# Gate and convolution tiles of a state-space group in turns, a planner that keeps TensorE to one kind of pass, and attention's output gates through DRAM between heads

## The chip, the cores and the metric

The kernel runs on one NeuronCore of a Trainium2 chip. The metric is device time in microseconds (us), from the start to the end of one execution. Engines are named as in the profile: PE is TensorE, DVE is VectorE, ACT is ScalarE, POOL is GpSimd, SP is SyncE, which issues most DMAs.

## The reference, cut to what matters

One layer of a hybrid encoder: 16 learned rows are put ahead of 512 tokens, and an attention branch and a bidirectional state-space (SSD) branch run on the same normalized rows. Every input-side column comes from one projection with `w_in`.

```python
u = rmsnorm(h, norm_w)                                   # 528 x 1024
q_lat, kv_lat, k_rope, g_attn, z, xbc, dt_raw, merge = split(u @ w_in)
y_a = mla_branch(q_lat, kv_lat, k_rope, ...)             # 16 heads, softmax over 528 keys
y_a = (y_a * silu(g_attn)) @ w_attn_proj
xbc = silu(conv5(xbc) + conv_b)                          # x, B, C of 4 groups of 8 heads
y = ssd_fwd(x, dt, B, C) + ssd_bwd(x, dt, B, C) + d_skip * x
y = rmsnorm(y * silu(z))                                 # by group
y_s = y @ w_ssd_proj
gates = sigmoid(merge)                                   # 2 x 1024 columns
h = h + (gates[0] * y_a + gates[1] * y_s) @ w_out
out = rmsnorm(h, final_norm_w)[16:]
```

## The kernel before, in words

Everything is float32. A projection is split in three: weights and inputs are cut into a high and a low part of type `fp32r`, and hi*hi, hi*lo and lo*hi are added up in PSUM (`proj`). Such a matmul goes through PE in one pass. A few matmuls of the SSD part (`cb`, `st`, `yo`, `yd`, `ssq`) are plain float32; each shows up in the trace as two MATMUL records. Transposes are a third kind (`tr`, `pt`, `yt`, `rb`).

The work is written as generators, "units". A projection unit loads 512 KB of weights (`wr`), lets ACT cast the high part (`wh`) and DVE form the low part (`wl`), then runs 24 matmuls of 512 columns into one PSUM bank, or 48 of 270 for a convolution tile. The units that matter here:

- `silu_tile` makes a gate tile `z` (SSD groups: `z_units`; attention: `g_fill`).
- `conv_tile` makes B, C or one of four x tiles of a group (`in_units`): a projection into a two-bank PSUM tile of tag `d`, of which there are two, then five DVE operations over 528 columns.
- `proj_unit` multiplies a finished group by `w_ssd_proj` into `ysacc`.
- `merge_s` makes the SSD branch's output gate (`ms`), `merge_a` attention's (`ma`); each is a projection unit with a tanh behind it.
- `mix_unit` multiplies attention's output by `w_attn_proj`, applies the two gates and splits the sum for `out_unit`, the last projection.

The SSD groups run as main work: `ssd_tok`, `ssd_cb`, `ssd_state`, `ssd_cross`, `ssd_y`, `ssd_weight` and the epilogue `group_epi` (gating, norm, split of the group). Attention runs head by head: `score_gen` does four score tiles (`sc`, 24 matmuls), the row maximum on DVE, the exponential on ACT and the scaling on DVE; `value_gen` transposes the probabilities (`pt`, 20), splits them (`pT`, ACT then DVE) and multiplies them by the values (`o`, 9).

What fills PE around the main work stands in `queue`; `drive` opens up to four units of it at a time, in the queue's order as far as their conditions allow. This recording is then put in order by `_Recorder.order` (L164), a list scheduler with modelled durations: of all operations that can go it takes the one with the earliest modelled start, and among equals the one recorded first (`rank`). It charges 95 ns (`SWITCH`) whenever PE changes between a plain float32 matmul (`four`) and anything else. The instructions are emitted in that order, each engine runs its own in order, and all carry the line of `rec.emit` (L261).

The lines that the change touches: L210 to 212, the choice of the next operation; L1507 to 1512, which queue for each group first all z units, then all `proj_unit`s of the group before, then all convolution tiles of the next group; L1283 to 1292, `merge_a`, which leaves each gate in an SBUF slot; L1536, which queues the eight `merge_a` units for when head 13 (`GATES`) is done.

Of the kernel before, what the change touches and what calls it, by code (L numbers as in the profile page):

```python
# [9 lines left out]
F32 = mybir.dt.float32  # L10
# [6 lines left out]
P = 128  # L17
D = 1024
NM = 16
NX = 512  # L20
# [23 lines left out]
LAG = 1250.0  # L44
MAHEAD, TOKC, CBC = 2, 2, 1
MAINS, OPEN, LOOK = 24, 4, 20
QLATE, GATES, SPLIT = 1, 13, 99


WPOOL, WPOOLB = 2, 4  # L50
# [41 lines left out]
class _Recorder:  # L92
# [15 lines left out]
    @classmethod  # L108
    def region(cls, ap):
        step = ap.ap[0][0]  # L110
        if ap.name == "cum_rows":
            return 0, 1, [(0, 1)]
        p0, f0 = divmod(ap.offset, step) if step else (0, ap.offset)
        dims = [(st, n) for st, n in ap.ap[1:] if st and n > 1]
        if "PSUM" in str(getattr(ap, "space", "")):
            end = f0 + sum(st * (n - 1) for st, n in dims)
            return 0, P, [(f0 // cls.BANK * cls.BANK, (end // cls.BANK + 1) * cls.BANK)]
        dims.sort(reverse=True)
        spans = [(f0, f0 + 1)]
        for k, (st, n) in enumerate(dims):  # L120
            rest = sum(a * (b - 1) for a, b in dims[k:]) + 1
            inner = sum(a * (b - 1) for a, b in dims[k + 1:]) + 1
            if inner >= st or n * len(spans) > 32:
                return p0, p0 + ap.shape[0], [(a, a + rest) for a, _ in spans]
            spans = [(a + st * m, a + st * m + 1) for a, _ in spans for m in range(n)]
        return p0, p0 + ap.shape[0], spans
# [31 lines left out]
        o.tiles = sorted({n for n, _ in rs + ws if n in self.tags})  # L158
        self.ops.append(o)

    AHEAD, SPARE = 4, 2
    TO_PE, TO_REST, SWITCH = 155.0, 35.0, 95.0

    def order(self):  # L164


        ops = self.ops
        left, ready = [0] * len(ops), [0.0] * len(ops)
        for o in ops:
            o.succs = []  # L170
        for o in ops:
            for k in o.preds:
                ops[k].succs.append(o)
            left[o.i] = len(o.preds)
        count, last, held, place, turn, passed = {}, {}, set(), {}, {}, {}
        for o in ops:
            for n in o.tiles:
                if n not in count:
                    tag = self.tags[n]
                    place[n] = turn.get(tag, 0)  # L180
                    turn[tag] = place[n] + 1
                count[n] = count.get(n, 0) + 1
        turn = {t: 0 for t in turn}
        passed = {t: set() for t in turn}
        free = {t: [0.0] * self.cap[t] for t in turn}
        clk = {e: 0.0 for e in ("PE", "DVE", "ACT", "POOL", "SP")}
        cand = {e: [] for e in clk}
        port = lock = wire = 0.0
        four = False
        for o in ops:  # L190
            if not left[o.i]:
                cand[o.eng].append(o)

        def when(o):
            t = max(clk[o.eng], ready[o.i], lock if o.eng == "POOL" else port if o.both else 0.0)
            for n in o.tiles:
                if n not in held:
                    tag = self.tags[n]
                    f, ahead = free[tag], place[n] - turn[tag]
                    if not f or ahead > self.AHEAD or (ahead > 0 and len(f) <= self.SPARE):  # L200
                        return None
                    t = max(t, f[0])
            return t

        out = []
        while len(out) < len(ops):
            best = None
            for q in cand.values():
                for o in q:
                    t = when(o)  # L210
                    if t is not None and (best is None or (t, o.rank) < best[:2]):
                        best = (t, o.rank, o)
            if best is None:
                raise RuntimeError(("no operation can go", len(out)))
            t, _, o = best
            cand[o.eng].remove(o)
            o.start = t
            for n in o.tiles:
                if n not in held:
                    held.add(n)  # L220
                    tag = self.tags[n]
                    free[tag].pop(0)
                    passed[tag].add(place[n])
                    while turn[tag] in passed[tag]:
                        turn[tag] += 1
            more = 0.0
            if o.eng == "PE" and o.four != four:
                four, more = o.four, self.SWITCH
            elif o.both:
                lock = t + o.occ  # L230
            elif o.eng == "POOL":
                port = t + o.occ + 60.0
            if o.eng == "SP":
                clk["SP"] = t + 420.0
                wire = max(wire, t + 1600.0) + o.dur
                end = wire + o.extra
            else:
                clk[o.eng] = t + o.occ + more
                end = t + o.dur + more
            for n in o.tiles:  # L240
                last[n] = max(last.get(n, 0.0), end + 40.0)
                count[n] -= 1
                if not count[n]:
                    f = free[self.tags[n]]
                    f.append(last[n])
                    f.sort()
            for s in o.succs:
                to = end + (self.TO_PE if s.eng == "PE" else self.TO_REST) if s.preds[o.i] else t + o.occ
                ready[s.i] = max(ready[s.i], to)
                left[s.i] -= 1  # L250
                if not left[s.i]:
                    cand[s.eng].append(s)
            out.append(o)
        self.span = max(o.start + o.dur for o in out)
        return sorted(out, key=lambda o: (o.start, o.i))
# [98 lines left out]
def hybrid_block_kernel(ctx, tc, a, out):  # L354
    nc = tc.nc
    scr = nc.dram_tensor("cum_rows", (2, NC, 32, P), F32, kind="Internal").ap()

    cp = ctx.enter_context(tc.tile_pool(name="cp", bufs=1))
    rp = ctx.enter_context(tc.tile_pool(name="rp", bufs=WRAW))
# [438 lines left out]
    def has(*keys):  # L798
        return lambda: all(k in done for k in keys)
# [478 lines left out]
        done.add(("ms", m))  # L1278

    w_ap = a["w_attn_proj"][0].rearrange("(k p) m -> p k m", p=P)  # L1280
    mx_, gates, ysp = {}, {}, {}

    def merge_a(m):  # L1283
        w = yield from w_cols(O_MA + m * P)
        ps = yield from proj(w, u_src, QRY)
        wdone()
        yield
        z = slot([P, NX], name="ma")
        A.activation(z, ps, AF.Tanh, scale=0.5)
        drop("m")  # L1290
        gates[m] = z
        done.add(("ga", m))

    def split_y(p):
# [7 lines left out]

    def mix_unit(m):
        w = yield from weights(lambda raw: [(raw, w_ap[:, :, m * P:(m + 1) * P])], KD, P)
        ps = yield from proj(w, [ysp[p] for p in range(KD)], slice(0, NX))
        wdone()
        yield has(("ga", m), ("ms", m))
        z = gates.pop(m)
        V.scalar_tensor_tensor(z, z, 1.0, ps, op0=ALU.add, op1=ALU.mult)
        drop("m")  # L1310
        tt(V, z, z, ysacc[:, m, :], ALU.add)
        yield
        h = slot([P, NX], F32R, name="mxh")
        l = slot([P, NX], F32R, name="mxl")
        A.copy(h, z)
        yield
        lo_of(V, l, z, h)
        mx_[m] = (h, l)
        done.add(("mx", m))
# [117 lines left out]
    def fill(makes, cond=None):  # L1437
        for mk in makes:
            queue.append(Item(mk, cond))
# [22 lines left out]
    def epi_ok(g):  # L1462
        return g < 0 or ("epi", g) in done
# [31 lines left out]
    for g in range(NG):  # L1495
# [8 lines left out]
        main(lambda g=g: ssd_tok(g), lambda g=g, pv=pv: core_in(g) and "dt" in done and pv(("yd", g - 1, TOKC)))  # L1504
        main(lambda g=g: ssd_cb(g), lambda g=g, pv=pv: ("in", g, 0) in done and ("in", g, 1) in done and pv(("yd", g - 1, CBC)))
        main(lambda g=g: group_epi(g), lambda g=g: has(("yd", g, 3), *[("z", g, ti) for ti in range(4)])())
        if g:  # L1507
            fill(z_units(g))
        if g:
            proj_fill(g - 1)  # L1510
        if g + 1 < NG:
            in_fill(g + 1)
    fill([mark(lambda t=t: ql_unit(t), ("ql", t)) for t in range(3)])
    fill([mark(lambda t=t: kvl_unit(t), ("kvl", t)) for t in range(2)])
    fill([lambda: lat_norm("q", NX, QL, qnw)], lambda: all(("ql", t) in done for t in range(3)))
# [9 lines left out]
    for p in range(KD):  # L1525
        if p % 2 == 0:
            fill([lambda p=p: pe_unit(p // 2)], lambda p=p: lat_ok() and score_ok(2 * p - 3))
        fill([lambda p=p: q_unit(p), lambda p=p: k_unit(p)], lambda p=p: "att" in done and lat_ok() and score_ok(2 * p - 2))
        if p % 2 == 0:
            fill([lambda p=p: v_unit(p // 2)], lambda p=p: lat_ok() and (p == 0 or ("A", 2 * p - 3) in done))  # L1530
        if p == 0:
            proj_fill(3)
        fill([lambda p=p: merge_s(p)], lambda p=p: ("proj", 3, p // 2) in done)
        if p + 1 < KD:
            g_fill(p + 1)
    fill([lambda m=m: merge_a(m) for m in range(KD)], lambda: ("A", GATES) in done)  # L1536
    for h in range(NH):
        main(lambda h=h: score_gen(h), lambda h=h: ("q", h) in done and ("k", h) in done
             and (h < 1 or ("P", h - 1) in done) and (h < 2 or ("A", h - 2) in done))
# [47 lines left out]
```

## Time and profile before

| | |
|---|---|
| median of 3 runs | 912.46 us (910.71 to 915.15) |
| profiled execution: its own time, its span | 913.33 us, 911.5 us |
| busy: PE, DVE, ACT | 878.5 us (96%), 707.9 us (78%), 543.2 us (60%) |
| DMA | 83.3 MB, mean 91 GB/s |

The span runs from the first to the last instruction. Matmuls are pipelined, and a MATMUL record lasts some 0.16 us longer than the time until the next one may start, so PE's busy time overstates its work: time lost on PE is the distance from start to start, less the spacing that the same matmuls have when nothing holds them up.

In order of time the span is: start and the first inputs (0 to 75 us), four SSD groups (to about 475), the latents and the last SSD projections (to 540), 16 heads (to 804), the mix with `w_attn_proj` and the output (to the end).

### The profile page before, as it was taken

How to read it: one execution, taken by the hardware profiler on the slowest of the kernel's cores; microseconds unless marked ns; L12 is line 12 of the kernel's file. 1: busy time of each engine (PE TensorE's matmuls, PEld its weight loads, DVE VectorE, ACT ScalarE, POOL GpSimd, SP SyncE). 2: the span in 40 equal slices, each digit the busy share in tenths (PEclk: the TensorE clock that was granted, in tenths of full speed). 3: DMA queues.
4: the chain of work that ended last, by engine and by line, in shares of the span. 5: the costliest groups of instructions: out<-in, count | busy, mean ns of one | idle time of the engine just before them, and what ended most of it. 6: DMA issues, size and time to landing. Idle time of an engine off the chain costs nothing.

```text
span 911.5 us, 13243 instructions
## 1 busy us (share of the span) xinstructions
PE 878.5 (96%) x4984; PEld 725.7 (80%) x4984; DVE 707.9 (78%) x1245; ACT 543.2 (60%) x1159; POOL 11.7 (1%) x20
## 2 busy tenths in 40 slices
PE   7999999999989999999999999999999999999997
PEld 5997878867878769977788888877777878888885
DVE  6798799968799689979768757969989897334464
ACT  6369469965776447855344556757777685432232
POOL 1000000000000000000001000000000000000000
PEclk9999999999999999999999999999999999999998
DMA  7254246434524236332224333121121001433322
GB/s 219 71 165 119 70 120 166 109 93 113 141 70 139 70 84 160 104 116 70 70 70 102 81 87 92 38 53 29 38 50 33 15 24 47 135 121 101 104 70 92
DMA packets 126952, 83.30 MB, mean 91 GB/s; under 512 B 26354, under 2 KB 114071, under 8 KB 126889
## 3 DMA queue, kind: packets, MB, share of 16 engines
q1 hardware_dynamic: 126709, 82.33, 33.3%
q8 instruction: 39, 0.64, 0.3%
q14 instruction: 24, 0.20, 0.1%
q10 hardware_dynamic: 180, 0.14, 0.0%
HBM read 80.22 MB, written 2.23 MB: 90 GB/s over the span
## 4 chain that ended last, share of the span: by engine, by line
PE 74%; DVE 17%; ACT 4%; issue 2%; DMA 1%; POOL 0%; POOLq 0%; ACTq 0%; DVEq 0%
PE pj L261 53%; PE wo L261 4%; PE sc L261 3%; PE st L261 2%; PE yo L261 2%; PE o L261 2%; DVE x L261 2%; DVE wl L261 2%; PE pt L261 2%; PE tr L261 2%; PE yd L261 1%; DVE mx L261 1%; DVE pT L261 1%; DVE yo L261 1%; DVE C L261 1%
## 5 line engine op out<-in xcount | busy, mean ns | idle before, releaser
L261 PE MATMUL pj<-uh,wh 128*128 128x512 f32 (+3 forms) x776 | 158.8, 346 | 8.0 <-DVE yo L261 3.5
L261 DVE TENSOR_TENSOR wl<-wr,wh 128x1024 fp32r<-128x1024 f32 (+1 forms) x102 | 123.9, 1217 | 53.2 <-ACT wh L261 53.0
L261 PE MATMUL pj<-uh,wl 128*128 128x270 f32 (+3 forms) x776 | 157.1, 339 | 0.0
L261 PE MATMUL pj<-ul,wh 128*128 128x270 f32 (+3 forms) x776 | 150.0, 335 | 0.0
L261 ACT CAST wh<-wr 128x1024 fp32r<-128x1024 f32 (+1 forms) x102 | 106.3, 1042 | 63.1 <-PE pj L261 41.3
L261 PEld LDWEIGHTS pj<-uh,wh 128*128 128x128 f32 (+1 forms) x776 | 121.9, 191 | 27.6 <-issue 5.1
L261 PEld LDWEIGHTS pj<-ul,wh 128*128 128x128 f32 (+1 forms) x776 | 122.6, 189 | 15.0
L261 PEld LDWEIGHTS pj<-uh,wl 128*128 128x128 f32 (+1 forms) x776 | 122.0, 190 | 13.2 <-issue 0.2
L261 ACT ACTIVATE ar<-ar,nacs 128x128 f32<-128x128 f32 x256 | 80.8, 391 | 24.5 <-DMA ar<-cum_rows 19.3
L261 PE MATMUL sc<-kst,qst 96*128 96x264 f32 (+1 forms) x384 | 67.2, 299 | 6.3 <-ACT p L261 5.4
L261 PEld LDWEIGHTS sc<-kst,qst 96*128 96x128 f32 (+1 forms) x384 | 53.6, 189 | 11.7 <-ACT p L261 8.6
L261 ACT ACTIVATE p<-sc,mx 128x528 f32<-128x528 f32 x64 | 45.3, 707 | 21.3 <-DVE mx L261 20.8
L261 PE MATMUL pt<-cst,p 128*128 128x128 f32 (+1 forms) x320 | 52.2, 274 | 1.4 <-DVE pT L261 0.8
L261 DVE TENSOR_TENSOR pT<-pt,pT 128x512 fp32r<-128x512 f32 x64 | 43.8, 685 | 11.5 <-ACT pT L261 11.3
L261 PE MATMUL o<-pT,v 128*128 128x512 f32 x128 | 46.6, 417 | 3.5 <-ACT pT L261 2.9
L261 DVE SCALAR_TENSOR_TENSOR x<-pj,chv,x 128x528 f32<-128x528 f32 x64 | 48.8, 763 | 0.8 <-ACT x L261 0.3
L261 PEld LDWEIGHTS pt<-cst,p 128*128 128x128 f32 (+1 forms) x320 | 37.3, 130 | 12.7 <-DVE p L261 1.5
L261 DVE TENSOR_REDUCE mx<-sc 128x1 f32<-128x528 f32 x64 | 44.6, 698 | 2.2 <-PE sc L261 1.9
L261 ACT CAST pT<-pt 128x512 fp32r<-128x512 f32 x64 | 37.3, 587 | 14.6 <-PE pt L261 14.4
L261 ACT ACTIVATE w<-cbm,dt_t 128x128 f32<-128x128 f32 x128 | 39.9, 390 | 2.9 <-DVE cbm L261 2.9
L261 PE MATMUL pj<-nh,wh 128*128 128x512 f32 x128 | 39.6, 431 | 0.0
L261 DVE SCALAR_TENSOR_TENSOR w<-cbm,dt_t,w 128x128 f32<-128x128 f32 x128 | 38.1, 347 | 0.0
(224 smaller groups left out, 1467.2 us busy)
## 6 DMA issues: line engine op xcount, KB each, us to landing
wr<-in_w_in SPq DMA_DIRECT2D x69, 512.0 KB, 4.0
ar<-cum_rows SPq DMA_DIRECT2D x32, 512.0 KB, 5.3
wr<-in_w_ssd_proj SPq DMA_DIRECT2D x16, 512.0 KB, 3.4
wr<-in_w_attn_proj SPq DMA_DIRECT2D x8, 512.0 KB, 3.6
wr<-in_w_out SPq DMA_DIRECT2D x8, 512.0 KB, 3.7
ws<-in_w_uq SPq DMA_DIRECT2D x36, 64.0 KB, 3.3
xt<-in_x SPq DMA_DIRECT2D x4, 512.0 KB, 5.3
fin<-in_x SPq DMA_DIRECT2D x4, 512.0 KB, 6.0
```

The costliest lines, as they stand in the source:

```text
L261: o.fn(*o.args, **o.kw)
```

## The change

Four edits. The queue of a group takes turns: z, conv, z, conv, z, conv, z, conv, `proj_unit`, conv, `proj_unit`, conv, two more `proj_unit`s. The scheduler adds 30 to the rank of a PE operation of the other kind (`STAY`), so that among PE operations with the same modelled start it stays with float32 or with the rest. `merge_a` stores its gate to a DRAM tensor (SP queue), and `mix_unit` loads it back ahead of its projection. The `merge_a` unit of pair p may go once head 2p+1 is done, and is queued between the units of the heads; the last one may go after head 14.

```diff
@@ _Recorder.order
-                    if t is not None and (best is None or (t, o.rank) < best[:2]):
-                        best = (t, o.rank, o)
+                    if t is None:
+                        continue
+                    r = o.rank + (self.STAY if o.eng == "PE" and o.four != four else 0)
+                    if best is None or (t, r) < best[:2]:
+                        best = (t, r, o)
@@ merge_a
         A.activation(z, ps, AF.Tanh, scale=0.5)
         drop("m")
-        gates[m] = z
+        yield
+        S.dma_start(gate_scr[m], z)
         done.add(("ga", m))
@@ mix_unit
         w = yield from weights(lambda raw: [(raw, w_ap[:, :, m * P:(m + 1) * P])], KD, P)
+        yield has(("ga", m))
+        z = slot([P, NX], name="ga")
+        S.dma_start(z, gate_scr[m])
         ps = yield from proj(w, [ysp[p] for p in range(KD)], slice(0, NX))
         wdone()
-        yield has(("ga", m), ("ms", m))
-        z = gates.pop(m)
+        yield has(("ms", m))
@@ the queue of group g
-        if g:
-            fill(z_units(g))
-        if g:
-            proj_fill(g - 1)
-        if g + 1 < NG:
-            in_fill(g + 1)
+        todo = {"z": [(mk, None) for mk in z_units(g)] if g else [],
+                "p": [(mark(lambda m=m, g=g: proj_unit(g - 1, m), ("proj", g - 1, m)), lambda g=g: epi_ok(g - 1)) for m in range(4)] if g else [],
+                "i": [(mark(u, ("in", g + 1, i)), lambda g=g: epi_ok(g - 1)) for i, u in enumerate(in_units(g + 1))] if g + 1 < NG else []}
+        for k in "zizizizipipipp":
+            if todo[k]:
+                mk, cond = todo[k].pop(0)
+                fill([mk], cond)
@@ the queue of attention
         fill([lambda p=p: merge_s(p)], lambda p=p: ("proj", 3, p // 2) in done)
+        if p:
+            fill([lambda p=p: merge_a(p - 1)], lambda p=p: ("A", 2 * p - 1) in done)
         if p + 1 < KD:
             g_fill(p + 1)
-    fill([lambda m=m: merge_a(m) for m in range(KD)], lambda: ("A", GATES) in done)
+    fill([lambda: merge_a(KD - 1)], lambda: ("A", NH - 2) in done)
```

The first PE instruction that stands elsewhere is a projection of the first group, some 50 us into the span. PE runs the same 4744 matmuls before and after; changes between plain float32 and anything else in its order go from 119 to 83, and stretches of `yd` matmuls (float32 with a 64-column tile) from 25 to 28.

**PE, the end of head 9.** The names: `o` are value matmuls, `pt` transposes, `sc` score matmuls of the heads that follow. Before:

```order
L261 MATMUL o_1192<-pT_1206,v_1122 128x512 x2
L261 MATMUL pt_1213<-cst,p_1172 128x128 x2
L261 MATMUL pt_1213<-cst,p_1179 128x128 x2
L261 MATMUL sc_1215<-kst_812,qst_811 128x264 x6
L261 MATMUL o_1192<-pT_1210,v_1131 128x512
L261 MATMUL pt_1222<-cst,p_1172 16x128 x2
L261 MATMUL pt_1222<-cst,p_1179 16x128 x2
L261 MATMUL sc_1230<-kst_812,qst_811 128x264
L261 MATMUL pt_1226<-cst,p_1201 128x128
L261 MATMUL o_1192<-pT_1210,v_1131 128x512
L261 MATMUL pt_1226<-cst,p_1201 128x128
```

Of the change, the same place (`o_1211` is head 9's output there, `pj_1257` the projection of a `merge_a` unit):

```order
L266 MATMUL sc_1251<-kst_808,qst_807 128x264 x3
L266 MATMUL o_1211<-pT_1232,v_1162 128x512
L266 MATMUL sc_1251<-kst_808,qst_807 128x264 x3
L266 MATMUL pj_1257<-uh,wh_1252 128x512 x2
L266 MATMUL pt_1247<-cst,p_1234 128x128
L266 MATMUL pj_1257<-uh,wh_1252 128x512 x2
L266 MATMUL o_1211<-last_813,v_1166 128x512
L266 MATMUL pj_1257<-uh,wh_1252 128x512 x3
L266 MATMUL pt_1247<-cst,p_1234 128x128
L266 MATMUL pj_1257<-uh,wh_1252 128x512
L266 MATMUL pj_1257<-uh,wl_1253 128x512 x4
L266 MATMUL pt_1258<-cst,p_1220 128x128 x2
```

Before, no projection of a unit stands between this head's matmuls and the next head's; now one does, in pieces. Heads 5, 7, 9 and 11 had none before and have one or two now; heads 14 and 15 had five between them, and two behind, and have one, and the first matmuls of `mix_unit` behind it.

**DVE, the end of the second SSD group.** `x_166` and `nl` belong to the epilogue of that group, `x_369` with `pj` to convolution tiles of the next group, `w` and `cbm` to that group's decay weights. Before:

```order
L261 SCALAR_TENSOR_TENSOR w_388_492<-cbm_483,dt_t,w_388_492 128x128 x3
L261 TENSOR_TENSOR wl_496<-wr_476,wh_495 128x1024
L261 SCALAR_TENSOR_TENSOR x_166_270<-x_166_270,chv,rb_490 128x512 x4
L261 SCALAR_TENSOR_TENSOR x_369_473<-pj_485,chv,x_369_473 128x528
L261 TENSOR_TENSOR nl_498<-x_166_270,nh_497 128x512
L261 SCALAR_TENSOR_TENSOR x_369_473<-pj_485,chv,x_369_473 128x528
L261 SCALAR_TENSOR_TENSOR x_369_473<-pj_475,x_369_473 128x528
L261 SCALAR_TENSOR_TENSOR x_369_473<-pj_485,chv,x_369_473 128x528
L261 TENSOR_TENSOR nl_501<-x_166_270,nh_500 128x512
L261 SCALAR_TENSOR_TENSOR x_369_473<-pj_485,chv,x_369_473 128x528
L261 TENSOR_TENSOR wl_503<-wr_499,wh_502 128x1024
```

Of the change, the same epilogue:

```order
L266 SCALAR_TENSOR_TENSOR x_328_432<-pj_486,x_328_432 128x528
L266 SCALAR_TENSOR_TENSOR x_166_270<-x_166_270,chv,rb_495 128x512 x4
L266 TENSOR_TENSOR nl_505<-x_166_270,nh_504 128x512
L266 TENSOR_TENSOR nl_508<-x_166_270,nh_507 128x512
L266 TENSOR_TENSOR nl_512<-x_166_270,nh_511 128x512
L266 TENSOR_TENSOR nl_514<-x_166_270,nh_513 128x512
L266 TENSOR_TENSOR wl_519<-wr_500,wh_518 128x1024
```

The last convolution tile is now done before the epilogue's scaling, where four stood open or to come; two `proj_unit`s and a z unit run on PE meanwhile.

**SP, the end of attention.** `gate_rows` is the DRAM tensor of the gates, `ga` their way back, `fin` the rows of `x` for the residual, `wr` weights. Of the change:

```order
L266 DMA gate_rows<-ma_1285_1391 128x512
L266 DMA wr_1322_1428<-in_w_attn_proj 128x8x128
L266 DMA fin_1307_1413<-in_x 128x1024
L266 DMA ga_1323_1429<-gate_rows 128x512
L266 DMA ga_1325_1431<-gate_rows 128x512
L266 DMA gate_rows<-ma_1303_1409 128x512
L266 DMA fin_1308_1414<-in_x 128x1024
L266 DMA fin_1309_1415<-in_x 128x1024
L266 DMA fin_1310_1416<-in_x 128x1024
L266 DMA wr_1331_1437<-in_w_attn_proj 128x8x128
L266 DMA ga_1337_1443<-gate_rows 128x512
```

Before, the same stretch held only the `fin` and `wr` loads; now gate stores, which wait for a tanh on ACT, stand ahead of weight loads in the same queue.

## Rows read from the trace of the kernel before

**Rows 1.** The page's head and part 1: busy time, share of the span.

```profile
span 911.5 us, 13243 instructions
PE 878.5 (96%) x4984; PEld 725.7 (80%) x4984; DVE 707.9 (78%) x1245; ACT 543.2 (60%) x1159; POOL 11.7 (1%) x20
```

**Rows 2.** Waits of PE, 75 to 475 us: who, for whom, us, times, longest.

```profile
PE pj L261 <- DVE yo L261: 3.5, 2, 2.0
PE pj L261 <- DVE x L261: 2.1, 1, 2.1
```

**Rows 3.** Waits of PE, 565 to 805 us.

```profile
PE sc L261 <- ACT p L261: 5.4, 9, 1.4
```

**Rows 4.** Stretches in attention: bounds, length, busy PE, PEld, DVE, ACT, POOL; clock; DMA.

```profile
636.20:647.40 11.20, 9.84 (x67) 7.98 (x66) 10.98 (x23) 9.52 (x22) 0.00 (x0) 1.00 0.27 66
647.40:667.40 20.00, 19.17 (x116) 16.40 (x117) 16.04 (x38) 13.01 (x33) 0.00 (x0) 1.00 0.03 8
667.40:676.70 9.30, 7.84 (x54) 6.45 (x52) 8.52 (x17) 7.83 (x16) 0.00 (x0) 1.00 0.42 90
...
767.70:804.60 36.90, 36.90 (x183) 30.30 (x183) 14.49 (x20) 15.18 (x25) 0.00 (x0) 1.00 0.44 129
sum 239.10, PE 227.11 PEld 189.48 DVE 191.41 ACT 161.12 POOL 0.00; mean PE 16.22 PEld 13.53 DVE 13.67 ACT 11.51 POOL 0.00
```

**Rows 5.** The same columns for three stretches of the SSD groups.

```profile
105.00:160.00 55.00, 53.02 (x373) 45.31 (x371) 52.84 (x97) 38.06 (x103) 0.00 (x0) 0.97 0.49 131
...
235.00:285.00 50.00, 46.27 (x366) 43.79 (x365) 43.94 (x69) 34.10 (x77) 1.01 (x1) 1.00 0.38 101
...
322.00:371.00 49.00, 47.49 (x356) 40.98 (x354) 46.16 (x82) 33.39 (x87) 0.00 (x0) 1.00 0.51 129
```

**Rows 6.** PE in order of time, 264 to 274 us: start, length, idle before.

```profile
267.99 2.11 PE L261 MATMUL pj<-uh,wh 128*128 128x512 f32 x8 [1.59 <-ACT wh L261]
272.24 1.27 PE L261 MATMUL pj<-uh,wh 128*128 128x270 f32 x8 [2.14 <-DVE x L261]
```

**Rows 7.** PE in order of time, around a plain float32 matmul (`st`).

```profile
93.58 0.62 PE L261 MATMUL pj<-ul,wh 128*128 128x512 f32 x2
94.04 1.02 PE L261 MATMUL st<-xw,bt 128*128 128x512 f32 x2
94.90 0.60 PE L261 MATMUL tr<-cst,x 128*128 128x128 f32 x4
95.26 0.37 PE L261 MATMUL pj<-uh,wh 128*128 128x270 f32 x1
```

**Rows 8.** PE around a short and a long run of `yd`; a stretch of 270-column projections.

```profile
147.60 0.92 PE L261 MATMUL pj<-ul,wh 128*128 128x270 f32 x6
148.45 0.66 PE L261 MATMUL yd<-w,xtk 128*64 128x128 f32 x8
149.03 0.52 PE L261 MATMUL pj<-uh,wh 128*128 128x270 f32 x2
...
249.82 0.54 PE L261 MATMUL pj<-ul,wh 128*128 128x270 f32 x3
250.30 1.09 PE L261 MATMUL yd<-w,xtk 128*64 128x128 f32 x16
251.32 0.39 PE L261 MATMUL pj<-uh,wh 128*128 128x270 f32 x1
...
350.58 6.04 PE pj L261 x48
```

**Rows 9.** From the page: the low-part split of a weight tile.

```profile
L261 DVE TENSOR_TENSOR wl<-wr,wh 128x1024 fp32r<-128x1024 f32 (+1 forms) x102 | 123.9, 1217 | 53.2 <-ACT wh L261 53.0
```

**Rows 10.** DMA issues: count, KB each, median us from issue to landing.

```profile
wr<-in_w_in SPq DMA_DIRECT2D x69, 512.0 KB, 4.0
out<-fo SPq DMA_DIRECT2D x8, 256.0 KB, 2.2
fw<-in_final_norm_w SPq DMA_DIRECT2D x2, 256.0 KB, 4.3
```

More of the change, by code (lines that the diff above doesn't have):

```diff
@@ L46 @@
 MAINS, OPEN, LOOK = 24, 4, 20
-QLATE, GATES, SPLIT = 1, 13, 99
+QLATE, SPLIT = 1, 99
 WPOOL, WPOOLB = 2, 4
@@ L112, in region @@
             return 0, 1, [(0, 1)]
+        if ap.name == "gate_rows":
+            return 0, 1, [(ap.offset // (P * NX), ap.offset // (P * NX) + 1)]
         p0, f0 = divmod(ap.offset, step) if step else (0, ap.offset)
@@ L159, in add @@
         self.ops.append(o)
-    AHEAD, SPARE = 4, 2
+    AHEAD, SPARE, STAY = 4, 2, 30
     TO_PE, TO_REST, SWITCH = 155.0, 35.0, 95.0
@@ L356, in hybrid_block_kernel @@
     scr = nc.dram_tensor("cum_rows", (2, NC, 32, P), F32, kind="Internal").ap()
+    gate_scr = nc.dram_tensor("gate_rows", (KD, P, NX), F32, kind="Internal").ap()
     cp = ctx.enter_context(tc.tile_pool(name="cp", bufs=1))
@@ L1280, in hybrid_block_kernel @@
     w_ap = a["w_attn_proj"][0].rearrange("(k p) m -> p k m", p=P)
-    mx_, gates, ysp = {}, {}, {}
+    mx_, ysp = {}, {}
     def merge_a(m):
```

## The prediction, on record before the run

> **What bounds the kernel now.** I read the page's head first [rows 1]: PE is busy 96% of the span, DVE 78%. PE runs the same matmuls before and after the change, so only the time that PE loses can change: waits, and what a change of matmul shape costs. The start-to-start spacing of undisturbed matmuls gives the work: 0.23 us for 512 columns (two in 0.46 [rows 7]), 0.126 for 270 (48 in 6.04 [rows 8]), about 0.12 for the 264 of a score half, and 0.11 for a transpose (0.60 for four, whose last record runs on some 0.27 [rows 7]). Counting all 4984 records at such spacings leaves about 54 us lost. Some 13 of it lie in the first 75 us, which the change hardly touches, 19 in the SSD groups, 22 in heads 1 to 13; heads 14 and 15 and all behind them lose nothing.
>
> Attention decides, so I read it head by head, from one head's first value matmul to the next one's. A head's own work is 24 score matmuls (2.9 us), 20 transposes (2.2) and 9 value matmuls (2.1), 7.2 us; a projection unit adds 24 x 0.23 = 5.6; the smaller q, k, v and rope projections come in even heads, about 5.6. Elapsed time less this work, the loss per head: odd heads without a unit (5, 7, 9, 11) 2.5, 2.1, 1.7, 2.9; odd heads with one (1, 3, 13) 2.2, 2.7, 1.4; even heads with one, 2 to 12, 0.7, 0.6, 1.6, 0.3, 1.9, 1.1; heads 0, 14 and 15, with two or more each, 0. Head 7 shows how [rows 4]: 9.3 us for 7.2 of work, DVE busy 8.5 of them; head 5 has DVE busy 10.98 of 11.2. DVE is the bound there, and what PE then waits for by name is the exponential that stands behind DVE's row maximum [rows 3]. In head 6, with one unit and the small projections, DVE is busy 80%. In heads 14 and 15 DVE is busy 14.5 of 36.9 us: the eight `merge_a` units sit where DVE has little to do. Over all these heads DVE has 191.4 us of work in 239.1 [rows 4]. (The 12 us of PE idle in that sum are the smaller reading, since each record overlaps the next start.)
>
> In the SSD groups PE's longer waits are few: 3.5 us for the bank that a `yo` must leave, 2.1 for one that a convolution must leave [rows 2], 1.6 for a weight cast [rows 6]. They fall where convolution tiles meet other DVE work: DVE is busy 96%, 88% and 94% in the three stretches with such a cluster [rows 5].
>
> **The change part by part.**
>
> Staying with one kind of pass. The scheduler's price is 95 ns; 36 changes fewer would be 3.4 us. The rows show none of it: `st` starts 0.46 after two projections of 0.23, lasts 2 x 0.43, and four transposes and the next projection follow at their own spacing [rows 7]. I take 0. What does cost is the narrow tile: ahead of `yd` the spacing grows by 0.09 (six projections, 0.85 instead of 0.76), eight records take 0.58 and sixteen 1.02, so one run cut in two costs 2 x 0.58 - 1.02 + 0.09 = 0.23, and with the slower first matmul behind it (0.1) about 0.33 [rows 8]. Three runs more: +0.7 to +1.0, taken +0.9. The Trainium skill, in TensorEngine Tiling (Array Packing), section Key Properties, says that changing the tiling mode, not just the tile, drains TensorE; the `yd` rows agree. By it the order of passes is worth nothing and every additional mode change costs; it counts ten more of them here where I charge three runs, some 1.7 us at half a run's 0.33 each.
>
> The group's queue in turns. At the end of the second group PE lost 1.59 + 2.14 us [rows 6] because four convolution tiles and the epilogue shared DVE. In the new order the epilogue stands behind the last convolution tile, and `proj_unit`s, with about half the DVE work, run meanwhile. Against it: convolution tiles now run beside `yo` matmuls in the second group too, on the same two banks, as in the first and third, where such a mix lost about 2.0 and 1.5 of the 3.5 us [rows 2]. The first cluster stays as it is. So -3.7 there, +1.7 for the new mix, sum -2; bounds -6 (all but the first wait goes) and +3 (a second wait like the first).
>
> The gates between heads. A unit brings DVE 1.22 us of splitting [rows 9] and PE 5.6. An odd head's DVE work (8.5 in head 7, which holds a split already [rows 4]) is then at most 9.7 on 12.8 us of PE work, 76%; head 5's 11 makes 12.2 on some 14, 87%. That is an even head's share, so I take an even head's loss, 1.0 (mean of the six). Heads 1, 7, 9, 11, 13: 5.0. Heads 3 and 5 have two units in the new order: as heads 0 and 14, 0. Even heads, no longer starting behind a starved one: 0.8 each, 4.8. Heads 14 and 15 have one unit and then only 14 matmuls of `mix_unit` (3.2 us) as cover: 1.5 each. Sum 12.8 in place of 21.6, -8.8. Bounds: odd heads lose as those with one unit do today (2.1 x 5), even heads keep their 6.2, 14 and 15 lose 2.1 each: 20.9, -0.7. Or every head with a unit loses nothing, as head 0, and the end 2: -19.6. The value is nearest the row of DVE's share, since the units now stand in pieces between scores and transposes.
>
> The way through DRAM. Each store and load is 256 KB; such a store landed in 2.2 us, such a load in 4.3 [rows 10]. Eight of each add 4 MB to 83. A load is issued ahead of its projection of 5.6 us and needed behind it: hidden. If the cover were gone, the last gate, issued within its own projection, could be 1 us late; the 12 output matmuls behind it (2.8) cover the chain, so 0, bound +1. The last head's chain to the first mix product, four DVE and ACT steps of 0.5 to 0.7, is 2.5 to 3 us against 11 matmuls, 2.6: +0.3. The stores stand in SP's queue; behind each are weights needed a unit or more later, so 0, with its price under the rivals. The three `x` loads at the end stand ahead of the fourth mix weight, which PE needs some 20 us later by its order: hidden.
>
> Sum: 0.9 - 2 - 8.8 + 0.3 = -9.6. Against the profiled execution's 913.33 us (its span and 1.8 around it) that is 903.7; the median of the runs shown is 0.9 lower, so **903 us**.
>
> **The rivals.** *Spreading moves the loss and doesn't remove it.* Odd heads with one unit lose 2.1 today, hardly less than those with none (2.3); DVE and ACT would bound each stretch of scores and transposes alone, whatever stands around it. For it speak heads 1, 3 and 13; against it that their unit stood in one block, before or behind the stretch that lost. Then attention gives 0.7 to 3, and with the other terms the time is 908 to 912.
>
> *The balance fills completely.* Every head behaves as heads 0, 14 and 15, or the SSD waits all go: 890 to 898. Against it: even heads with a unit and the small projections still lose 1.0.
>
> *SP's queue turns against it, slower.* A gate store waits for a tanh, and the queue behind it for the store: late weights (4.0 us to land [rows 10], 1.22 for the split [rows 9], about as much for the cast ahead of it) stall PE. It decides when a store goes out less than some 6.5 us ahead of the next weight tile's first matmul; eight stores at 2 us each are 16, which outweighs the 9.6, and gives 919. Against it: the order has a weight tile loaded more than a unit ahead, and SP's waits today are mostly for buffers.
>
> *A pass kind does cost.* The scheduler's 95 ns were right where I could not see it: 3.4 us more, 899 to 900, within the forecast's own range.
>
> **How the numbers follow.** Forecast, 898 to 908: 0.62. Fills completely, 890 to 898: 0.12. Spreading does nothing, 908 to 912: 0.18. Slower by SP's queue or a bare end: 0.08. From no change this kernel's measurement can tell about 0.5%, 4.6 us, so faster means under 907.9 and slower over 917.0. Faster: 0.60 of the forecast, the 0.12, and 0.02 of the third, 0.74. Slower: 0.06 of the last. The rest, 0.20, is the same. The range leaves out a tenth at each end: 893 to 911.
>
> **What would show it.** Right: elapsed time of heads 7, 9 and 11 near 14 us, with DVE busy about 85%; no wait over 1 us in heads with a unit; DVE's share over heads 14 and 15 well above 39%; no wait of 1.6 and 2.1 at the end of the second group; `st` and `yo` starting at their neighbours' spacing. The prediction is wrong if odd heads with a unit still lose 2 us, if heads 14 and 15 lose more than 5 together, if weight loads land late behind gate stores, or if the convolution tiles beside `yo` bring waits over 2 us in every group.

## The result and the profile after

The changed kernel takes 897.79 us (median of 4 runs, 896.62 to 899.38) against 912.48, a ratio of 0.9838 (95% interval 0.9808 to 0.9867): 14.7 us faster, where 9.5 were forecast (903 against 912.46). A second series of runs of both kernels gave the same ratio (0.9838, 0.9814 to 0.9862).

The page's head and part 1 of the changed kernel, beside [rows 1]:

```profile
span 896.7 us, 13288 instructions
PE 875.1 (98%) x4984; PEld 723.3 (81%) x4984; DVE 707.8 (79%) x1245; ACT 544.2 (61%) x1159; POOL 13.3 (1%) x20
```

The work is the same, and the span is 14.8 us shorter. PE's lost time, counted over the 4984 records as in the prediction (distance from start to start less the spacing of an undisturbed record of that shape), says where that came from. A head is counted from its first value matmul to the next head's.

| stretch, us lost | before | after | change | forecast |
|---|---|---|---|---|
| 0 to 75 us | 12.7 | 12.4 | -0.4 | - |
| 75 to 200 us | 7.0 | 5.6 | -1.4 | the SSD groups together: |
| 200 to 330 us | 7.3 | 4.9 | -2.4 | -2 for the turns, |
| 330 to 475 us | 5.1 | 6.2 | +1.1 | +0.9 for the narrow tile |
| to the first value matmul | 0.8 | 0.4 | -0.4 | - |
| heads 0 to 15 | 21.5 | 8.3 | -13.3 | -8.8 |
| behind them | -0.3 | 0.5 | +0.8 | +0.3 |

The sum is -16.0; the first matmul of the profiled execution came 1.2 us later, which leaves the 14.8.

By head, before and after: head 0 lost nothing and loses 0.6, head 1 lost 2.2 and loses 0.8, head 3 2.7 and 0.1, head 5 2.5 and 0.3, head 7 2.1 and 0.2, head 9 1.7 and 0.6, heads 11 and 12 together 4.0 and 1.0; the even heads 2 to 10 went from 5.1 to 1.4 together. Heads 13, 14 and 15 went the other way, from 1.3 to 3.3. The stretches that answer to [rows 4] are heads 5, 6, 7, 9 and 11, and heads 14 and 15 together:

```profile
634.90:653.50 18.60, 18.60 (x102) 15.27 (x101) 14.19 (x26) 11.79 (x23) 0.00 (x0) 1.00 0.28 70
653.50:673.80 20.30, 20.30 (x129) 17.84 (x128) 16.29 (x36) 14.04 (x32) 0.00 (x0) 1.00 0.18 50
673.80:687.50 13.70, 13.70 (x84) 11.38 (x83) 11.99 (x24) 10.92 (x24) 0.00 (x0) 1.00 0.29 64
705.10:719.20 14.10, 14.01 (x84) 11.62 (x83) 12.77 (x26) 10.68 (x22) 0.00 (x0) 1.00 0.13 37
737.90:752.70 14.80, 14.69 (x90) 12.30 (x89) 12.84 (x29) 11.93 (x26) 0.00 (x0) 1.00 0.16 45
783.80:800.70 16.90, 15.85 (x90) 12.47 (x89) 10.70 (x18) 10.11 (x18) 0.00 (x0) 1.00 0.52 172
```

Heads 7, 9 and 11 last 13.7, 14.1 and 14.8 us, with DVE busy 88, 91 and 87%; "near 14" and "about 85%" were the forecast. What is new is the second column: PE is busy for the whole of head 7. DVE at 88% goes with a loss of 0.2 us there.

PE's waits in attention, where [rows 3] had 5.4 us in nine for the exponential (546 to 805 us):

```profile
PE pj L266 <- DVE pT L266: 1.0, 2, 0.9
PE o L266 <- DVE pT L266: 0.5, 1, 0.5
PE sc L266 <- DVE kst L266: 0.3, 1, 0.3
PE sc L266 <- ACT p L266: 0.2, 1, 0.2
```

And in the SSD groups, 75 to 475 us, beside [rows 2]:

```profile
PE pj L266 <- DVE yo L266: 2.6, 3, 2.0
PE pj L266 <- DVE x L266: 1.6, 1, 1.6
```

The 2.0 for `yo` is the first cluster's, as before. The second group's two waits [rows 6] are gone. The 1.6 for `x` is new, at 389 us, at the end of the third group, ahead of a 512-column projection. The three stretches of [rows 5]:

```profile
105.00:160.00 55.00, 53.02 (x380) 45.22 (x380) 54.18 (x98) 40.01 (x104) 0.00 (x0) 1.00 0.50 134
235.00:285.00 50.00, 50.00 (x320) 44.17 (x320) 45.23 (x74) 39.56 (x89) 1.07 (x1) 1.00 0.40 118
322.00:371.00 49.00, 48.58 (x332) 41.52 (x331) 48.42 (x90) 39.73 (x105) 0.00 (x0) 1.00 0.61 161
```

In the second, DVE is busier than before (45.2 us for 43.9) and PE doesn't wait at all. The gates' way, by the DMA issues:

```profile
wr<-in_w_in SPq DMA_DIRECT2D x69, 512.0 KB, 3.9
gate_rows<-ma SPq DMA_DIRECT2D x8, 256.0 KB, 2.0
ga<-gate_rows SPq DMA_DIRECT2D x8, 256.0 KB, 4.4
```

They land as the neighbouring rows said (2.2 and 4.3). That time counts from the issue and leaves out what an issue waits in the queue. SP's waits for the tanh ahead of a gate store, and the one wait for a weight tile (`wr`) that the profile shows on PE, ACT or DVE:

```profile
SPq L266 <- ACT ma L266: 58.1, 7, 10.8
ACT wh L266 <- DMA wr<-in_w_in: 1.7, 1, 1.7
```

So the queue does stand for up to 10.8 us behind a store, and the weight tiles come early enough all the same: before the change ACT waited for one three times, 2.8 us together.

### The profile page after: what moved, and what is told of

Same layout as the page of the kernel before. It is cut to its first block, busy times and chain, and to the rows that moved or that the text cites. A ratio compares the mean times of both kernels' runs of the same rounds, so it can differ in the third digit from the quotient of the medians.

```text
span 896.7 us, 13288 instructions
## 1 busy us (share of the span) xinstructions
PE 875.1 (98%) x4984; PEld 723.3 (81%) x4984; DVE 707.8 (79%) x1245; ACT 544.2 (61%) x1159; POOL 13.3 (1%) x20
## 4 chain that ended last, share of the span: by engine, by line
PE 84%; DVE 9%; ACT 3%; issue 1%; DMA 1%; POOL 0%; POOLq 0%; SPq 0%; ACTq 0%; DVEq 0%
PE pj L266 58%; PE sc L266 4%; PE wo L266 4%; PE pt L266 3%; PE o L266 3%; PE yo L266 2%; PE st L266 2%; PE yd L266 2%; PE tr L266 2%; PE v L266 2%; DVE wl L266 2%; DVE B L266 1%; DMA ar<-cum_rows 1%; DVE C L266 1%; PE yt L266 1%
## 5 line engine op out<-in xcount | busy, mean ns | idle before, releaser
L266 PE MATMUL pj<-uh,wh 128*128 128x270 f32 (+3 forms) x776 | 161.2, 345 | 5.8 <-DVE x L266 3.1
L266 PE MATMUL pj<-uh,wl 128*128 128x270 f32 (+3 forms) x776 | 158.9, 338 | 0.0
L266 ACT ACTIVATE ar<-ar,nacs 128x128 f32<-128x128 f32 x256 | 81.6, 390 | 16.7 <-DMA ar<-cum_rows 16.6
L266 PE MATMUL sc<-kst,qst 96*128 96x264 f32 (+1 forms) x384 | 64.6, 296 | 1.0 <-DVE kst L266 0.3
L266 PEld LDWEIGHTS pt<-cst,p 128*128 128x128 f32 (+1 forms) x320 | 37.2, 130 | 12.4 <-DVE p L266 1.1
```

Source lines behind the costliest of these rows:

```text
L266: o.fn(*o.args, **o.kw)
```

## The experiments

The theory after the result: each part acts in its own stretch, and units between the heads fill PE there. Against it stood that the parts help one another, that a pass kind does cost, and that the gates' way alone freed something. Times below are medians with the ratio to the kernel before, measured on the same chip.

| kernel | us | ratio, 95% interval |
|---|---|---|
| gates alone | 900.0 | 0.986 (0.9839 to 0.9882) |
| gates through DRAM, still behind head 13 | 914.22 | 1.0019 (1.0008 to 1.003) |
| turns alone | 913.52 | 1.0014 (1.0002 to 1.0027) |
| STAY alone | 915.76 | 1.0033 (1.0022 to 1.0044) |
| the whole change, again | 898.64 | 0.9838 (0.9814 to 0.9862) |
| the change without STAY | 898.87 | 0.984 (0.9815 to 0.9866) |
| yd gathered, all float32 held back | 908.97 | 0.9947 (0.9927 to 0.9966) |
| the unit of head 11 left out | 901.41 | 0.9865 (0.9843 to 0.9888) |
| the narrow tile alone charged | 896.03 | 0.9811 (0.9786 to 0.9836) |
| the same, other turns | 893.09 | 0.9777 (0.9752 to 0.9802) |

**The gates alone.** The kernel before with the change's whole hunks of `merge_a`, `mix_unit` and the queue of attention, of which the core is

```diff
-        gates[m] = z
+        yield
+        S.dma_start(gate_scr[m], z)
...
+        if p:
+            fill([lambda p=p: merge_a(p - 1)], lambda p=p: ("A", 2 * p - 1) in done)
```

> The kernel before with the gates' part alone: store and load through DRAM, and the units of merge_a between the heads. Theory (each part acts in its own stretch, and the units between the heads fill PE there): -12 to -13.5 us, about 899.5; the lost time of heads 0 to 15 falls from 21.6 to about 8.5, and the SSD groups keep the 19.5 they lose before. The forecast's own term was -8.5, 904. Rival (the other two edits help in the heads as well, through the order that they leave): less than -9 here.

-12.7 us, within the theory's range. The heads lose 7.2 us instead of 21.5, and the SSD groups 18.0 instead of 19.4, all of the difference between 75 and 200 us (a matter of the clock, last section). By the medians nearly the whole result is this part; by the profiles all of it: behind the first 75 us the changed kernel loses only some 0.3 us less than this one (16.7 in the SSD groups, but 8.3 in the heads).

**The gates' way alone.** The kernel with the gates alone, and the old queue in it:

```diff
-        if p:
-            fill([lambda p=p: merge_a(p - 1)], lambda p=p: ("A", 2 * p - 1) in done)
...
-    fill([lambda: merge_a(KD - 1)], lambda: ("A", NH - 2) in done)
+    fill([lambda m=m: merge_a(m) for m in range(KD)], lambda: ("A", GATES) in done)
```

> The kernel before with the gates through DRAM, but all eight units of merge_a still behind head 13, so that only the way of the gates changes. Theory: the way costs nothing and brings nothing, -0.5 to +1 us, 912 to 913.5, and odd heads 5, 7, 9 and 11 still lose 2 us each. Rival (the gate slots in SBUF held up other units, and freeing them was the gain): -3 us or more, with less loss in heads 12 to 15. Second rival (gate stores hold up the SP queue): +2 us or more.

+1.5 us (interval 0.7 to 2.7): 0.5 above the theory's range, 0.5 short of the second rival's, which the time alone doesn't exclude. The first rival fell: nothing was gained, and the heads lose 21.5 us as before, head by head within 0.1. What the profile has more is 1.5 us between 475 and 545 us, partly at half the clock (last section), and there no gate has been stored yet: the first goes behind head 13. The way through DRAM brings nothing by itself; whether its 1.5 us are the clock alone stays open.

**The turns alone.** The kernel before with the change's hunk of the group's queue, whose order is

```diff
+        for k in "zizizizipipipp":
```

> The kernel before with the queue of the SSD groups in turns alone. Theory: the waits of 1.6 and 2.1 us at the end of the second group go, three more runs of yd cost 1.0: -1 to -3 us, 909.5 to 911.5, all of it between 75 and 475 us. Rival (the gain between 75 and 475 us came from keeping to one kind of pass): 0 to +2, 912.5 to 914.5.

+0.8 us by the medians (1.0014): the sign was missed. The second group gains what was expected (4.6 us lost between 200 and 330 us, instead of 7.3), and two other places take it back. The third group loses 7.3 instead of 5.1, with the same new wait as in the changed kernel. Its row, PE in order of time:

```profile
389.89 2.10 PE L261 MATMUL pj<-uh,wh 128*128 128x512 f32 x8 [1.61 <-DVE x L261]
```

And the heads lose 23.5 instead of 21.5: the turns bring projections forward that had filled head 0 (two units there before, none now), and head 2 loses 2.3 instead of 0.7. PE's wait for the exponential from 565 to 805 us, which was 5.4 in nine:

```profile
PE sc L261 <- ACT p L261: 6.3, 11, 1.0
```

**STAY alone.** The kernel before with

```diff
+                    r = o.rank + (self.STAY if o.eng == "PE" and o.four != four else 0)
+                    if best is None or (t, r) < best[:2]:
+                        best = (t, r, o)
```

> The kernel before with STAY alone: 81 changes of the kind of pass instead of 119, 26 runs of yd instead of 25. Theory (a change of kind costs nothing, a narrow run 0.33): 0 to +0.5 us, 912.5 to 913. Rival (95 ns a change): -3.6 us, 908.9.

+3.0 us, on the far side of the theory, and 6.9 from the rival that prices a change of kind: 38 changes fewer, and slower. The stretch from 200 to 330 us loses 10.1 us instead of 7.3. Both waits of [rows 6] are still there, and a third has come; PE in order of time:

```profile
266.98 2.11 PE L264 MATMUL pj<-uh,wh 128*128 128x512 f32 x8 [1.91 <-ACT wh L264]
270.83 1.28 PE L264 MATMUL pj<-uh,wh 128*128 128x270 f32 x8 [1.74 <-DVE x L264]
292.77 0.33 PE L264 MATMUL tr<-cst,x 128*128 128x128 f32 x1 [1.10 <-DVE x L264]
```

The third wait is 1.1 of the 2.8; the rest is in pieces too small to name. Another 1.1 us is lost between 475 us and the first value matmul.

**The change without STAY**, beside the whole change:

```diff
-    AHEAD, SPARE, STAY = 4, 2, 30
+    AHEAD, SPARE = 4, 2
...
-                    r = o.rank + (self.STAY if o.eng == "PE" and o.four != four else 0)
-                    if best is None or (t, r) < best[:2]:
-                        best = (t, r, o)
+                    if t is not None and (best is None or (t, o.rank) < best[:2]):
+                        best = (t, o.rank, o)
```

> The changed kernel as it is, for the comparison with the three beside it. Ratio to before 0.982 to 0.986, 896 to 899.5 us; the granted clock stands at 0.5 less often than in the kernel before.

> The changed kernel with STAY = 0, so that turns and gates are left: 117 changes of the kind of pass instead of 83, the same 28 runs of yd. Theory (a change of kind costs nothing; STAY's 3 us alone were a new wait of DVE in the second group, which the turns take away): within 1 us of the changed kernel. Rival (95 ns a change of kind): 3.2 us slower than the changed kernel.

0.2 us between the two, whose ratios are 0.984 and 0.9838: the theory held. The runs of the two differ in clock (0.997 to 0.999 without STAY, 0.996 to 0.998 with it), so the medians alone could hide a microsecond or two; but the profiles, from 75 us on, lose the same within 0.2 us. 117 or 83 changes of kind make no difference that shows, and in company with the turns STAY does no harm.

**Gathering the narrow tile.** The scheduler counts three kinds instead of two, and stays longer:

```diff
-    AHEAD, SPARE, STAY = 4, 2, 30
+    AHEAD, SPARE, STAY = 4, 2, 200
...
-        four = False
+        four = 0
...
-                         four=self.name == "PE" and op != "transpose" and not kw.get("is_transpose") and lhs.dtype == F32)
+                         four=0 if self.name != "PE" or op == "transpose" or kw.get("is_transpose") or lhs.dtype != F32 else 2 if cols == 64 else 1)
```

> The changed kernel, whose scheduler takes a 64-column float32 matmul for a kind of its own and adds 200 to the rank instead of 30: 15 runs of yd instead of 28, 71 changes of kind instead of 83. Theory (each run saved is worth 0.33 us, changes of kind nothing): 3 to 4.5 us faster than the changed kernel, about 894, as far as holding back other work brings no new wait. Rival (the narrow tile costs by the matmul, not by the run): within 1 us. Second rival (each operation held back is late for DVE): slower.

The price was right and the time wrong. In this trace eight records of `yd` between undisturbed neighbours cost 0.79 us, sixteen 1.18 to 1.22, 32 2.10: 0.055 a record and 0.345 a run. PE in order of time around a run of 32:

```profile
209.52 1.18 PE L266 MATMUL pj<-ul,wh 128*128 128x270 f32 x8
210.63 1.97 PE L266 MATMUL yd<-w,xtk 128*64 128x128 f32 x32
212.53 1.98 PE L266 MATMUL yo<-h,C 128*128 128x512 f32 x4
```

13 runs saved are 4.5 us, but the kernel is 10.3 slower than the changed one beside it. Its longest waits from 75 to 500 us:

```profile
PE pj L266 <- DVE yo L266: 4.6, 5, 1.9
PE ssq L266 <- DVE sq L266: 4.3, 3, 2.3
PE pj L266 <- DVE ql L266: 2.3, 1, 2.3
PE st L266 <- DVE xw L266: 1.4, 3, 0.6
```

The second rival held, as far as the waits go: PE now waits for what DVE makes of `yo`, and ahead of `ssq` and `st`. That DVE had stood idle before, because they were held back, is argued and not shown; the experiment with the narrow tile alone speaks for it. And not all of the 10.3 us are waits. This kernel ran at a lower clock (0.989 to 0.996, median 0.9925; the changed one beside it 0.9965), and its profile has two stretches at half the clock, the first 2 us behind a wait and the second begun in one (columns as in [rows 4]):

```profile
279.50:282.90 3.40, 3.40 (x12) 2.70 (x11) 1.44 (x3) 0.48 (x1) 0.12 (x1) 0.50 0.05 13
487.70:494.60 6.90, 6.00 (x17) 4.77 (x17) 5.71 (x11) 2.21 (x6) 1.52 (x2) 0.51 0.00 0
```

The matmuls of these stretches took 4 us longer than at full clock (estimated from their spacings).

**A unit taken out of one head.** Of the changed kernel:

```diff
-        if p:
-            fill([lambda p=p: merge_a(p - 1)], lambda p=p: ("A", 2 * p - 1) in done)
+        if p and p != 6:
+            fill([lambda p=p: merge_a(p - 1 - (p > 6))], lambda p=p: ("A", 2 * p - 1) in done)
...
+    fill([lambda: merge_a(KD - 2)], lambda: ("A", NH - 3) in done)
     fill([lambda: merge_a(KD - 1)], lambda: ("A", NH - 2) in done)
```

> The changed kernel with the merge_a unit that stands in head 11 left out there, the later ones each one place on, and two behind head 13: head 11 has no unit and head 14 has two. Theory (what an odd head loses is the lack of a unit, about 2 us whatever DVE's share; heads 14 and 15 lose for lack of cover): head 11 loses 2 to 2.5 instead of 0.6, heads 14 and 15 together 0 to 0.5 instead of 1.7, time within 1 us of the changed kernel. Rival (the order of all pieces between the heads does it, not the unit in that head): head 11 loses under 1.

Half of it held. Head 11 loses 2.1 instead of 0.6, so a unit is worth what the theory said. Two things came that it did not say. Head 12, whose own work is unchanged, loses 1.3 instead of 0.45: a starved head hands on part of its lag. And heads 14 and 15 lose 1.6 instead of 1.7 although head 14 has two units, so the time is 2.8 us longer instead of the same. Heads 11, 12, and 14 with 15:

```profile
736.40:747.50 11.10, 9.88 (x70) 8.17 (x69) 9.77 (x22) 9.80 (x22) 0.00 (x0) 1.00 0.22 61
747.50:764.70 17.20, 16.45 (x94) 13.80 (x95) 15.49 (x30) 14.13 (x30) 0.00 (x0) 1.00 0.01 1
779.10:801.40 22.30, 21.39 (x113) 16.98 (x112) 11.98 (x18) 11.55 (x20) 0.00 (x0) 1.00 0.56 179
```

Head 11's DVE is busy 88% of the time, as in head 11 of the changed kernel with its unit (87%), and this one loses 2.1. DVE's share doesn't tell the two apart.

**The narrow tile alone.** What the traces price is charged, and nothing else: 170 ns where PE enters or leaves a `yd` run, and 60 on the rank.

```diff
-    AHEAD, SPARE, STAY = 4, 2, 30
-    TO_PE, TO_REST, SWITCH = 155.0, 35.0, 95.0
+    AHEAD, SPARE, STAY = 4, 2, 60
+    TO_PE, TO_REST, SWITCH = 155.0, 35.0, 170.0
...
-                         four=self.name == "PE" and op != "transpose" and not kw.get("is_transpose") and lhs.dtype == F32)
+                         four=self.name == "PE" and op != "transpose" and not kw.get("is_transpose") and lhs.dtype == F32 and cols == 64)
```

> The changed kernel, whose scheduler counts the 64-column tile alone as another kind of pass (170 ns a change, 60 on the rank) and leaves the other float32 matmuls where they fall: 17 runs of yd instead of 28, 111 changes between float32 and the rest. Theory (a run saved is worth 0.345 us, other changes nothing, and what made the earlier run with 15 yd runs slow was that st, yo and cb were held back, which DVE then waited for): 2 to 4 us faster than the changed kernel, 895 to 896.5, with no new wait over 1 us between 75 and 475 us. Rival (gathering yd itself starves DVE): slower than the changed kernel by 3 us or more, with new waits behind yd.

896.03 us, a ratio of 0.9811 where the changed kernel has 0.9838: 2.5 us better by the ratios, whose intervals overlap. 11 runs fewer are 3.8 us at 0.345, and the waits over 1 us stayed the changed kernel's two. What its 111 changes between float32 and the rest cost (83 in the changed kernel) can't be told from the 1.3 us that are missing from the 3.8.

**Other turns on top of it.** Of the kernel before it:

```diff
-    AHEAD, SPARE, STAY = 4, 2, 60
+    AHEAD, SPARE, STAY = 4, 2, 150
...
-    for k in "1a2345bcd":
+    for k in "1a2534cbd":
...
-        for k in "zizizizipipipp":
+        for k in ['iiiiii', 'iiizzzizpiippp', 'zizziiizppipip', 'zzzzpppp'][g]:
```

> As the run before it, with 150 on the rank, convolution tiles ahead in the turns of the second and third group, and the first group's z tiles in another order: 14 runs of yd. Theory: 3 to 6 us faster than the changed kernel, 892.5 to 895.5, as the waits of 2.1 and 1.8 us that it has left in the SSD groups get shorter too. Rival (three convolution tiles in a row meet the yo tiles on their two banks, as before the change): waits of 2 us come back in the second group and the time is that of the changed kernel or more.

893.09 us, 19.9 less than before (0.9777, 0.9752 to 0.9802), the best of all. The waits did not get shorter as expected; they moved (75 to 500 us):

```profile
PE pj L266 <- DVE yo L266: 3.2, 3, 2.4
PE ssq L266 <- DVE sq L266: 1.7, 1, 1.7
PE rb L266 <- DVE rc L266: 1.2, 1, 1.2
```

The 2.4 for `yo` is the first cluster's; the 1.7 for `ssq` is new, in the second group, and stays under the rival's 2. The gain is in the third group: 1.9 us lost between 330 and 475 us instead of 6.2, with the wait at 389 us gone, and 14 runs of `yd` in all. The heads are back at 7.2. Rank, turns and the first group's order went in together; what each is worth is not shown.

## Why the prediction was right, and where its sizes were off

**The range held and the direction was right**; the result lies 0.2 us below the forecast's own range of 898 to 908. By the time alone that is the edge of the rival that the balance fills completely (890 to 898), but the trace is not that rival's: the heads still lose 8.3 us and the SSD groups 16.7. The forecast put the gain in the heads 4.5 us too low, and 1.2 us of the result came from the clock, which it did not price.

**Gates between the heads (-8.8, measured -13.3 in the heads): the mechanism was right, the size wrong.** The step that failed is "that is an even head's share, so I take an even head's loss, 1.0". It took DVE's share for the cause of the loss. Heads 7, 9 and 11 stand at 87 to 91% and lose 0.2 to 0.6; head 11 without its unit stands at 88% and loses 2.1. It is the unit that matters: where PE has a projection to go on with, in pieces between scores and transposes, DVE may be nearly full. Head 13 shows how closely it must stand. It has a unit in both kernels and loses 1.4 before and 1.6 after, with DVE busy 92% in both; nearly all of that loss lies ahead of the unit's first projection. Its row (columns as in [rows 4]) before, then after:

```profile
753.60:767.70 14.10, 13.34 (x79) 10.97 (x78) 13.01 (x27) 9.42 (x20) 0.00 (x0) 1.00 0.15 38
```

```profile
768.70:783.80 15.10, 14.28 (x85) 11.66 (x84) 13.82 (x27) 9.92 (x20) 0.00 (x0) 1.00 0.20 70
```

PE's two waits in it and the unit's first matmuls, in the changed kernel:

```profile
772.84 0.49 PE L266 MATMUL o<-pT,v 128*128 128x512 f32 x1 [0.46 <-DVE pT L266]
775.05 0.33 PE L266 MATMUL pt<-cst,p 128*128 128x128 f32 x1 [0.21 <-DVE p L266]
776.60 0.63 PE L266 MATMUL pj<-uh,wh 128*128 128x512 f32 x2
```

The even heads of before were a poor model because part of their loss was the odd head's ahead of them. I allowed 0.2 of 1.0 for that; by the experiment with head 11 left bare it was 0.9. So the heads 2 to 12 with even numbers lose 1.8 together where 4.8 were taken, and 1, 7, 9, 11 and 13 lose 3.8 where 5.0 were. Heads 3 and 5 lose 0.4, where 0 was taken. The rival that the spreading only moves the loss fell with this.

**The end of attention (1.5 for each of heads 14 and 15, +0.3 behind: 3.3; measured 1.7 and 0.8 more behind).** The size is near, its reason was not lack of a unit. Head 15's loss is the last chain; PE in order of time in the changed kernel:

```profile
797.79 0.51 PE L266 MATMUL o<-pT,v 128*128 128x512 f32 x1
799.17 0.50 PE L266 MATMUL pj<-yah,wh 128*128 128x512 f32 x1 [0.87 <-DVE pT L266]
```

With two units in head 14 that wait remained.

**The turns (-2, bounds -6 and +3).** The two waits named went, and one new wait of 1.6 us came, near the 1.7 charged, but in the third group and not in the second, and ahead of a 512-column projection where a convolution tile beside `yo` had been charged: that the sizes agree is luck. Alone the turns cost 0.8 us. With the gates in place the ratios are 0.986 for the gates alone and 0.984 with the turns, some 2 us, less than the intervals can tell; and the gates alone ran at a lower clock (0.994 to 0.996) than the kernel without STAY (0.997 to 0.999). By the profiles of the gates alone and of the changed kernel the SSD groups gain 1.3 us by the rest of the change, and the heads lose 1.1 (7.2 without turns, 8.3 with them), because the turns take filler from the heads, which the prediction did not see. So a gain by the turns is not shown.

**Pass kind (0) and narrow tile (+0.9).** Both terms held. Without STAY the time is the same within what the clock leaves open, and a run costs 0.345 us where 0.33 was taken. The Trainium skill's rule of TensorEngine Tiling (Array Packing), section Key Properties, that a change of tiling mode drains TensorE, goes with the 0.345; no run here prices the transposes that change the tile too. What was not said is that an order chosen by a price that isn't there can cost of itself: STAY alone made the kernel 3.0 us slower, of which a new wait of 1.1 is named.

**DRAM and the SP queue (0).** The queue stands behind gate stores as the rival said (58.1 us in seven waits), yet nothing needed is late; that rival fell. The 1.5 us of the way alone are above the term's bound (+1), and not at the place that it named.

**What is left over.** 1.4 us of the SSD groups' gain, between 75 and 200 us, come from no term of the sum; 1.2 of it is the clock, as the last section shows.

## What to carry to other kernels

Look for stretches in which the engine that bounds the kernel has nothing to go on with, and give each a unit of its own; a starved stretch also slows the next, so it costs more than its own row shows. Whether another engine's busy share was 80 or 90% there said little here (88% in two heads, 0.2 and 2.1 us lost). Charge a list scheduler with prices that the trace shows (here 0.345 us for a run of the narrow tile, nothing for float32 against the rest), and time each tie-break alone and in company: two of the three parts here were slower alone and harmless in company.

## What the runs showed of the hardware

The granted clock of TensorE fell to 0.50 (1.2 of 2.4 GHz) in the middle of busy stretches, in some executions and not in others. In the profile of the kernel before it did so from 118.4 to 121.8 us, 0.3 us behind the end of PE's 1.98 us wait for `yo`; the same instructions stand at full clock in the changed kernel. First the stretch (columns as in [rows 4]) and then PE's row in order of time, in the kernel before:

```profile
118.40:121.80 3.40, 3.40 (x17) 3.40 (x16) 3.40 (x7) 0.61 (x1) 0.00 (x0) 0.50 0.84 254
```

```profile
118.10 1.94 PE L261 MATMUL pj<-uh,wh 128*128 128x270 f32 x8 [1.98 <-DVE yo L261]
```

The same two of the changed kernel:

```profile
119.00:122.20 3.20, 3.18 (x25) 3.18 (x26) 3.20 (x6) 0.62 (x1) 0.00 (x0) 1.00 1.04 265
```

```profile
119.02 1.28 PE L266 MATMUL pj<-uh,wh 128*128 128x270 f32 x8 [1.98 <-DVE yo L266]
```

17 matmuls in 3.4 us where 25 in 3.2 would make 26 or 27: at 0.126 each [rows 8] that is 1.2 of the table's 1.4 us. With the gates through DRAM and the old queue there were three such stretches in the profiled execution, two around the end of the waits near 118 and 268 us, the third at 484 us, where PE had last waited 0.23 us, ahead of a transpose:

```profile
484.00:487.20 3.20, 3.20 (x10) 2.44 (x11) 1.57 (x4) 0.63 (x1) 1.15 (x2) 0.50 1.05 236
```

```profile
483.97 1.12 PE L263 MATMUL rb<-cst,rc 128*128 128x128 f32 x4 [0.23 <-DVE rc L263]
```

It shows in the times as well. Of the 42 runs of the kernel before in the first two series of experiments, the 8 with a mean clock of 0.997 have a median of 911.6 us, the 3 with 0.992 one of 915.9: 0.85 us for each 0.001. Its median clock was 0.995; the changed kernel's ten runs have 0.996 to 0.998, the four of the gates alone 0.994 to 0.996. At that rate 0.0025 of clock would be some 2 us of the result. That is an upper bound: the mean also counts the end of the span, where the clock is at 0.50 behind the last matmul and costs PE nothing (906.9 to 911.5 us before, 893.4 to 896.7 after). The profiles themselves show the 1.2 us at 118 us. The turns alone and STAY alone ran at a higher mean clock (median 0.998) than the kernel before, so their orders may cost more than the 0.8 and 3.0 us by the medians. The cause isn't settled: the waits near 118 and 268 us stand in the kernel with STAY alone too, and its clock was 0.996 to 0.999.
